# The RWKV-7 scan of layer 1: operands kept in DRAM by step, products of keys and queries by row halves, corrected values copied, states added and then scaled

## The chip, the cores and the metric

One core of one Trainium2 chip runs the whole program. The metric is the device time of one execution in microseconds (us), from the first instruction to the last. The engines are TensorE (PE; its weight loads are listed apart as PEld), VectorE (DVE), ScalarE (ACT), GpSimd (POOL) and SyncE (SP, which here issues nearly all transfers). All of it is in float32; a float32 product counts as two matmul instructions in the profile.

## What is computed

Two layers run over 512 latent tokens and 256 context tokens of width 1024. Layer 0 is attention beside a gated recurrence; layer 1 is a bidirectional RWKV-7 mixer; each has an MLP behind it. The change lies in layer 1's scan over time, which for each of 16 heads and both directions is

```python
def step(s, inp):
    r_t, w_t, kk_t, b_t, k_t, v_t = inp
    sk = jnp.einsum('bhvk,bhk->bhv', s, kk_t)
    s = s * w_t[:, :, None, :] - sk[..., None] * b_t[:, :, None, :] + v_t[..., None] * k_t[:, :, None, :]
    return s, jnp.einsum('bhvk,bhk->bhv', s, r_t)
```

over the context first and then over the latents, forward and backward, with a 64x64 state per head. Only the latent outputs are kept.

## The kernel before

The 768 tokens are cut into 12 chunks of 64. Within a chunk the recurrence is solved in closed form: a 64x64 triangular system per head and direction is inverted, and the chunks follow one another through the states. `order` gives 12 steps; step i takes one chunk forward and one backward, the first four steps over the context, the other eight over the latents. A tile holds the two directions on the two halves of the partitions, and two heads (n) per channel block; there are 8 channel blocks, `kt` 0 to 7, in two groups of four.

**Preparation** (`tm_prep`, run for 8 channel blocks by `tm_pairs`) forms the scaled keys and update vectors (`KB`), the scaled removal keys and receptances (`ql`, `qc`) and the products that the inversion starts from (`L`), and stores them in DRAM: `kbr`, `qlr`, `qcr`, `ldr`, each as one transfer from all 128 partitions. The values go to `vdr` from `tm_values`.

**The scan** (`tm_scan`) runs `tm_step(i, kt)` for the 12 steps and 8 blocks, and between the blocks of step i one piece each of

- `tm_feed(i + 1)`: loads `KB`, `QZ` and `W` of the next step, multiplies `KB` by `QZ` (16 products, `QZ` being zero where the directions don't meet), masks the result into `G` (L1082), copies the query rows of `QZ` into `G` (L1089), and transposes `KB` into `KT`;
- `tm_invert(j)`: loads `XT` from `ldr` and runs 60 multiplications and additions on `zt` and `Z` (L1124, L1125), for j in (1, 2, 4) on POOL, else on DVE; `tm_below(j)` finishes the inversion with 32x32 products.

A block of a step is a chain of small products in one PSUM tile `sc`: `G` by `W` (values over states), ACT's copy `rh`, `XT` by `rh`, DVE's predicated copy of the corrected values back into `W` (L1182), `KT` by `W`, and DVE's scaling of that sum by the decay, added to the state that POOL has already scaled (`Sd`, L1204). After each group of four blocks ACT copies the new states into the next step's `W` (L1200). Latent steps then form the outputs from `G` by `W` and `QZ` by the states.

No one writes the order of the instructions by hand: the framework's scheduler lays each engine's stream out ahead of time from its own estimates. Each engine then runs its stream in order, and a transfer is issued when SP comes to it and its buffer is free. `KB` has room for one step (two tiles of a half), `QZ` for two steps, `W` for two.

Of the kernel before, what the change touches and what calls it, by code (L numbers as in the profile page):

```python
# [15 lines left out]
P = 128  # L16
# [18 lines left out]
class Net:  # L35
# [810 lines left out]
    def tm_pairs(self, vin, lw):  # L846
# [3 lines left out]
        with self.psum("l1e") as self.pq:  # L850
# [25 lines left out]
            dec = self.sb([P, NT], F32, "L", 2)[:, :2 * KT * 12].rearrange("p (d k i) -> p d k i", d=2, k=KT)  # L876
# [67 lines left out]
    def tm_prep(self, kt, lw):  # L944
# [49 lines left out]
        for d in range(2):  # L994
# [11 lines left out]
            nc.sync.dma_start(self.kbd[d, kt], KB)  # L1006
            ql, qc = self.sb([P, 8, 128], F32, "ql", 3), self.sb([P, 4, 64], F32, "qc", 3)
            (nc.vector if kt == KT - 1 else nc.gpsimd).tensor_mul(ql[:, :, 0:64], ch(kkn)[:, 0:8], eq[:, 0:8])
            nc.gpsimd.tensor_mul(qc, ch(kkn)[:, 8:], eq[:, 8:])
            nc.gpsimd.tensor_mul(ql[:, :, 64:128], ch(r), er[:, 0:8])  # L1010
# [3 lines left out]
            qs.append((ql, qc))  # L1014
# [5 lines left out]
            yield  # L1020
        for n in range(2):
            ps = self.mm2()
            h = half(n)
            for c in range(12):
                for d in range(2):
                    o = half(1 - d)
                    x, y = KBs[d][h, c, o], qs[d][0][h, c, 0:64] if c < 8 else qs[d][1][h, c - 8]
                    self.mm(ps[o, 64 * c:64 * c + 64], *((y, x) if d else (x, y)), True, True)
            L = self.sb([P, NT], F32, "L", 2)
            nc.scalar.activation(L, ps[:, :NT], AF.Copy)  # L1030
# [20 lines left out]

    def tm_feed(self, i, KB=None, W=None):

# [4 lines left out]
        m = 128 if lat else 64  # L1058
        KB = KB or [self.sb([P, 4, 2, 128], F32, "KB", 2) for _ in range(2)]
        W = f["W"] = W or self.sb([P, KT, 2, 2, 64], F32, "W", 2)  # L1060
        QZ = f["QZ"] = self.QZ[i % 2]
        by = lambda z: z.rearrange("k (n p) m -> p (k n) m", n=2)
        flat = lambda z: z.rearrange("p k n m -> p (k n) m")
        for d in range(2):
            h = half(1 - d)
            for g in range(2):
                nc.sync.dma_start(flat(KB[g][h]), by(self.kbd[d, 4 * g:4 * g + 4, :, cs[d]]))
            nc.sync.dma_start(flat(QZ[h, :, :, d, 0:m]), by(self.qld[d, :, :, cs[d]] if lat else self.qcd[d, :, :, cs[d] - 8]))
        for d in range(2):
            v = self.vd[64 * cs[d]:64 * cs[d] + 64].rearrange("t (k n v) -> t k n v", n=2, v=64)  # L1070
            nc.sync.dma_start(W[half(d), :, d], v)
        f["G"], f["KT"] = [], []
        yield
        for g in range(4):
            ps = self.mm2()
            for j in range(2):
                for n in range(2):
                    x = 2 * m * (2 * j + n)
                    self.mm(ps[:, x:x + 2 * m], KB[g // 2][:, 2 * (g % 2) + j, n], QZ[:, 2 * g + j, n, :, 0:m], True, True)
            G = self.sb([P, 2, 2, 2, m], F32, "G", 8)  # L1080
            f["G"].append(G)
            nc.vector.tensor_mul(G.rearrange("p k n d t -> p (k n) d t"),  # L1082
                                 ps[:, :8 * m].rearrange("p (k d t) -> p k d t", d=2, t=m),
                                 self.gmask[:, :, 0:m].unsqueeze(1).to_broadcast([P, 4, 2, m]))
            if i:

                for d in range(2):
                    h = half(1 - d)
                    nc.scalar.activation(G[h, :, :, d, 0:64], QZ[h, 2 * g:2 * g + 2, :, d, 0:64], AF.Copy)  # L1089
            yield  # L1090
        for g in range(2):
            ps = self.mm2()
            for j in range(4):
                for n in range(2):
                    x = 256 * j + 128 * n
                    nc.tensor.transpose(ps[:, x:x + 128], KB[g][:, j, n], self.ident)  # L1096
            T = self.sb([P, 4, 2, 128], F32, "KT", 3, pool=self.gp)
            nc.scalar.activation(T, ps.rearrange("p (k n x) -> p k n x", k=4, n=2), AF.Copy)
            f["KT"].append(T)
            yield  # L1100

    def tm_invert(self, j):
# [3 lines left out]
        XT = self.XT[j] = self.sb([P, 2, 2, KT, 64], F32, "XT", 3, pool=self.ip)  # L1106
        for s in range(2):
            for d in range(2):
                c = self.order[2 * j + s][d]
                h = self.half(1 - d)  # L1110
                nc.sync.dma_start(XT[h, s].rearrange("p n k t -> p (n k) t"),
                                  self.ld[:, :, h, 64 * c:64 * c + 64].rearrange("n k p t -> p (n k) t"))
            for b in range(2):
                nc.vector.copy_predicated(self.GL[:, 16 * s:16 * s + 16],
                                          self.pmask[:, b].unsqueeze(1).to_broadcast([P, 16, 32]),
                                          XT[:, s, :, :, 32 * b:32 * b + 32].rearrange("p n k t -> p (n k) t"))
# [10 lines left out]
    def tm_below(self, j):  # L1127
# [3 lines left out]
        XT = XA.rearrange("p s n k t -> p (s n k) t")  # L1131
# [3 lines left out]
        units = lambda z: z.rearrange("p (n k) t -> p n k t", n=2)  # L1135
# [23 lines left out]
    def tm_step(self, i, kt):  # L1159
# [5 lines left out]
        W = f["W"][:, kt]  # L1165
        XT = self.XT[i // 2][:, i % 2]
        Q = f["QZ"][:, kt]
        G = f["G"][kt // 2][:, kt % 2]
        K = f["KT"][g][:, j]
        S, Sd = self.S[g], self.Sd[g]  # L1170
        units = [(d, n) for n in range(2) for d in range(2)]
        pr = self.ps([P, 512], "sc", 4, pool=self.sps)
        col = lambda b, d: slice(128 * b + 64 * d, 128 * b + 64 * d + 64)
        for d, n in units:
            h = half(d) if first else slice(0, P)
            self.mm(pr[half(1 - d), col(0, n)], G[h, n, d, 0:64], W[h, d, n], True, True)
        rh = self.sb([P, 2, 64], F32, "rh", 4, pool=self.gp)
        nc.scalar.activation(rh, pr[:, 0:128].rearrange("p (n v) -> p n v", n=2), AF.Copy)
        for d, n in units:
            h = half(1 - d)  # L1180
            self.mm(pr[h, col(1, n)], XT[h, n, kt], rh[h, n], True, True)
        nc.vector.copy_predicated(W, self.umask.unsqueeze(2).unsqueeze(3).to_broadcast([P, 2, 2, 64]),  # L1182
                                  pr[:, 128:256].rearrange("p (n v) -> p n v", n=2).unsqueeze(1).to_broadcast([P, 2, 2, 64]))
        if not last:
            for d, n in units:
                self.mm(pr[half(1 - d), col(2, n)], K[:, n, half(1 - d)], W[:, d, n], True, True)
            if j == 0:
                self.S2 = self.sb([P, 4, 2, 64], F32, "S", 4, pool=self.gp)
            for n in range(2):
                m = self.dec[:, n, kt, i:i + 1]  # L1190
                if first:
                    nc.vector.tensor_scalar(self.S2[:, j, n], pr[:, col(2, n)], m, None, op0=OP.mult)
                else:
                    nc.vector.scalar_tensor_tensor(self.S2[:, j, n], pr[:, col(2, n)], m, Sd[:, j, n],  # L1194
                                                   op0=OP.mult, op1=OP.add)
            if j == 3:
                W2 = self.feeds[i + 1]["W"]
                for d in range(2):
                    h = half(1 - d)
                    nc.scalar.activation(W2[h, 4 * g:4 * g + 4, d], self.S2[h], AF.Copy)  # L1200
            if j == 3 and i < len(order) - 2:
# [326 lines left out]
```

## Time and profile before

| | us |
|---|---|
| median of 3 runs | 2262.69 (2258.92 to 2269.53) |
| profiled execution | 2269.31 |
| its span | 2267.5 |
| busy in the span: PE / PEld | 2023.4 / 1619.3 |
| busy in the span: DVE / ACT / POOL | 1145.4 / 869.6 / 519.6 |
| transfers of SP's queue, share of the 16 DMA engines | 36.8% |

The span divides into layer 0 and the projections of layer 1 (to about 1210 us), the preparation (to 1375), the last value products and the first inversions (to 1466), the scan's four context steps (to 1576) and eight latent steps (to 1816), the output projection (to 1905) and the last MLP. In a row of the profile "busy" is the union of the instructions of a group, "idle before" is the engine's idle time just ahead of them with what ended most of it, and PEclk is the clock that TensorE was granted (1.0 is its upper level, 2.4 GHz; 0.5 is 1.2 GHz).

### The profile page before, as it was taken

The page shows a single profiled execution, that of the slowest core. Times are in us where ns is not written, and L with a number is a line of the kernel's source. Part 1 is how long each engine was busy: PE and PEld are TensorE (multiplying, and loading weights), DVE is VectorE, ACT ScalarE, POOL GpSimd, SP SyncE. Part 2 cuts the span into 40 slices and gives each one's busy share as a digit, 9 for nine tenths or more (in the row PEclk, how much of TensorE's full clock was granted, in tenths as well). Part 3 has the DMA queues.
Part 4 walks back from the last instruction along what each step waited for, and adds up shares of the span by engine and source line. Part 5 has one row for each costly group of instructions (what it writes and reads, how often), then busy time and mean ns, then how long its engine had stood idle before and what let it go on. Part 6 is the DMA issues. An engine that isn't in the chain of part 4 may idle for free. (4 is left out here: it accounts for less than half of the span.)

```text
span 2267.5 us, 37320 instructions
## 1 busy us (share of the span) xinstructions
PE 2023.4 (89%) x15710; PEld 1619.3 (71%) x15710; DVE 1145.4 (51%) x1835; ACT 869.6 (38%) x1333; POOL 519.6 (23%) x530
## 2 busy tenths in 40 slices
PE   5888889999999999997987769779787778999999
PEld 3666547778888888875765449667676666888887
DVE  4556664342222222328647997648575684333333
ACT  3664454231121221317744543346454432232321
POOL 0122331010010100105004983661500220110110
PEclk8999999999999999998998778889898999999999
DMA  7324441123333122212224659396644440222222
GB/s 282 119 86 136 143 164 41 37 94 119 124 129 113 56 64 67 98 42 79 93 88 148 236 223 214 71 143 102 113 91 80 76 140 19 93 93 93 93 93 93
DMA packets 231944, 248.93 MB, mean 110 GB/s; under 512 B 52448, under 2 KB 209504, under 8 KB 225376
## 3 DMA queue, kind: packets, MB, share of 16 engines
q1 hardware_dynamic: 229728, 241.30, 36.8%
q0 software_dynamic: 896, 3.15, 0.4%
q8 instruction: 123, 2.02, 0.4%
q10 hardware_dynamic: 1152, 2.10, 0.2%
q14 instruction: 45, 0.37, 0.1%
HBM read 200.82 MB, written 41.94 MB: 107 GB/s over the span
## 5 line engine op out<-in xcount | busy, mean ns | idle before, releaser
L264 ACT ACTIVATE whi<-wst 128x1024 fp32r<-128x1024 f32 x160 | 169.2, 1059 | 587.3 <-PE mm L47 567.0
L47 PE MATMUL mm<-hhi,whi 128*128 128x512 f32 (+1 forms) x992 | 346.8, 356 | 16.2 <-ACT hhi L250 6.7
L47 PE MATMUL mm<-hlo,whi 128*128 128x512 f32 (+1 forms) x992 | 352.0, 356 | 3.6 <-DVE hlo L251 3.4
L47 PE MATMUL mm<-hhi,wlo 128*128 128x512 f32 (+1 forms) x992 | 349.6, 353 | 0.0
L265 DVE TENSOR_TENSOR wlo<-wst,whi 128x1024 fp32r<-128x1024 f32 x160 | 199.9, 1251 | 255.2 <-ACT whi L264 252.4
L345 POOL TENSOR_TENSOR mp<-mr 128x768 f32<-128x768 f32 (+1 forms) x64 | 109.9, 1719 | 848.1 <-ACT mr L344 848.1
L47 PE MATMUL mm<-ahi,wlo 128*128 128x512 f32 (+1 forms) x704 | 252.9, 359 | 0.0
L47 PE MATMUL mm<-ahi,whi 128*128 128x512 f32 (+1 forms) x704 | 252.9, 360 | 0.0
L47 PE MATMUL mm<-alo,whi 128*128 128x512 f32 (+1 forms) x704 | 252.5, 359 | 0.0
L300 DVE SCALAR_TENSOR_TENSOR Xt<-mm,mod,Xt 128x512 f32<-128x512 f32 (+1 forms) x112 | 70.6, 653 | 336.8 <-PE mm L47 336.6
L47 PEld LDWEIGHTS mm<-hhi,whi 128*128 128x128 f32 x992 | 187.8, 191 | 55.2 <-ACT hhi L250 8.7
L47 PEld LDWEIGHTS mm<-hlo,whi 128*128 128x128 f32 x992 | 188.9, 190 | 32.1 <-DVE hlo L251 6.6
L47 PEld LDWEIGHTS mm<-hhi,wlo 128*128 128x128 f32 x992 | 188.4, 190 | 28.3 <-issue 0.8
L47 PEld LDWEIGHTS mm<-ahi,whi 128*128 128x128 f32 x704 | 132.2, 188 | 28.1 <-issue 6.7
L47 PEld LDWEIGHTS mm<-ahi,wlo 128*128 128x128 f32 x704 | 132.5, 188 | 22.0 <-DVE wlo L265 1.1
L47 PEld LDWEIGHTS mm<-alo,whi 128*128 128x128 f32 x704 | 132.4, 188 | 21.9
L47 PE MATMUL mm<-QZ,KB 128*128 128x256 f32 (+1 forms) x384 | 96.4, 408 | 48.1 <-DMA QZ<-qlr 20.3
L47 PEld LDWEIGHTS mm<-QZ,KB 128*128 128x128 f32 x384 | 74.1, 227 | 60.3 <-issue 26.3
L347 DVE TENSOR_TENSOR alo<-mp,ahi 128x768 fp32r<-128x768 f32 (+1 forms) x64 | 54.9, 858 | 113.1 <-ACT ahi L346 113.0
L1082 DVE TENSOR_TENSOR G<-mm,gmask 128x1024 f32<-128x1024 f32 (+1 forms) x48 | 50.2, 1047 | 88.1 <-PE mm L47 87.8
L346 ACT ACTIVATE ahi<-mp 128x768 fp32r<-128x768 f32 (+1 forms) x64 | 47.3, 739 | 110.3 <-POOL mp L345 110.3
L47 PE MATMUL sc<-W,G 128*64 128x64 f32 (+1 forms) x1280 | 67.8, 233 | 12.8 <-DVE S L1194 10.3
(462 smaller groups left out, 4207.7 us busy)
## 6 DMA issues: line engine op xcount, KB each, us to landing
wst<-in_mlp_w_dram SPq DMA_DIRECT2D x64, 1024.0 KB, 5.4
wst<-in_ada_w_dram SPq DMA_DIRECT2D x48, 1024.0 KB, 6.4
kbr<-KB SPq DMA_DIRECT2D x16, 768.0 KB, 4.5
KB<-kbr SPq DMA_DIRECT2D x48, 256.0 KB, 5.6
wst<-in_rw_w_rkv_dram SPq DMA_DIRECT2D x8, 1024.0 KB, 5.4
qlr<-ql SPq DMA_DIRECT2D x16, 512.0 KB, 3.3
QZ<-qlr SPq DMA_DIRECT2D x16, 512.0 KB, 8.8
wst<-in_hy_w_in_dram SPq DMA_DIRECT2D x7, 1024.0 KB, 5.3
```

The source lines that it names most:

```text
L47: self.nc.tensor.matmul(out, lhsT, rhs, start=start, stop=stop)
L264: nc.scalar.activation(hi, w, AF.Copy)
L265: nc.vector.tensor_sub(lo, w, hi.bitcast(F32))
L300: self.nc.vector.scalar_tensor_tensor(x, ps[:, c0:c1], self.m(l, chunk, v, kt), x, op0=OP.mult, op1=OP.add)
L345: nc.gpsimd.tensor_mul(p[:, :n], r[:, :n], r[:, :n])
L346: nc.scalar.activation(h[:, :n], p[:, :n], AF.Copy)
L347: nc.vector.tensor_sub(o[:, :n], p[:, :n], h[:, :n].bitcast(F32))
L1082: nc.vector.tensor_mul(G.rearrange("p k n d t -> p (k n) d t"), ps[:, :8 * m].rearrange("p (k d t) -> p k d t", d=2, t=m), self.gmask[:, : ...
```

## The change

1. DRAM copies are laid out by step: `kbr`, `qkr` (removal keys of all 12 chunks), `qrr` (receptances of 8) and `ldr` hold one chunk's rows of one direction together, 4 or 8 KB per partition. The loads of a step become pieces of 4 KB; the stores become pieces of 512 B (`kbr`, `ldr`) and 256 B (`qkr`, `qrr`), and those of `kbr`, `qkr` and `qrr` are issued for each half of the partitions apart. `L` has one buffer that holds both heads' parts.
2. `QZ` is split in two tiles: `A` (two buffers; removal keys on one half, masked products on the other) and `R` (receptances, with zeros on the other half). `KB` is one tile for a step, with two buffers.
3. Products of keys and queries use one half of the rows each: 32 of 64x64 for `A`, and for latent steps 32 of 64x128 for `G`. ACT's copy of the query rows is gone.
4. The corrected values are copied by ACT for one half and DVE for the other.
5. States: DVE adds the new part to the state into `T`; after each group DVE scales one half and POOL the other into the next step's `W`, and POOL scales all of it into `S`.

```diff
-            nc.sync.dma_start(self.kbd[d, kt], KB)
+            for n in range(2):
+                nc.sync.dma_start(self.kbd[d, :, :, kt, n].rearrange("c p m -> p c m"), KB[half(n)])
...
-            nc.sync.dma_start(self.qld[d, kt], ql)
-            nc.sync.dma_start(self.qcd[d, kt], qc)
+            for n in range(2):
+                nc.sync.dma_start(self.qkd[d, :, :, kt, n].rearrange("c p m -> p c m"), qk[half(n)])
+                nc.sync.dma_start(self.qrd[d, :, :, kt, n].rearrange("c p m -> p c m"), qr[half(n)])
...
-            nc.sync.dma_start(self.ld[n, kt], L)
+        nc.sync.dma_start(self.ld[:, :, kt].rearrange("c p n t -> p c n t"), L)
...
-        KB = KB or [self.sb([P, 4, 2, 128], F32, "KB", 2) for _ in range(2)]
-        QZ = f["QZ"] = self.QZ[i % 2]
+        KB = self.sb([P, KT, 2, 128], F32, "KB", 2)
+        A = f["A"] = self.sb([P, 2, KT, 2, 64], F32, "A", 2)
+        R = f["R"] = self.R[i % 2]
...
+            h, c = half(1 - d), cs[d]
+            nc.sync.dma_start(A[h, d], self.qkd[d, c])
+            for g in range(0, KT, 4):
+                nc.sync.dma_start(KB[h, g:g + 4], self.kbd[d, c, :, g:g + 4])
...
-                    self.mm(ps[:, x:x + 2 * m], KB[g // 2][:, 2 * (g % 2) + j, n], QZ[:, 2 * g + j, n, :, 0:m], True, True)
+                    self.mm(ps[half(d), x:x + 64], KB[h, k, n, half(d)], A[h, d, k, n], True, True)
...
+                            self.mm(ps[:, x:x + 64], KB[h, 4 * g + j, n], R[h, d, 4 * g + j, n], True, True)
...
-        nc.vector.copy_predicated(W, ...
+        nc.scalar.activation(W[half(1), 0], by(pr[half(1), 128:256]), AF.Copy)
+        nc.vector.tensor_copy(W[half(0), 1], by(pr[half(0), 128:256]))
...
-                    nc.vector.scalar_tensor_tensor(self.S2[:, j, n], pr[:, col(2, n)], m, Sd[:, j, n],
-                                                   op0=OP.mult, op1=OP.add)
+                nc.vector.tensor_add(self.T[:, j], by(pr[:, 256:384]), S)
...
+            for d in range(2):
+                h = half(1 - d)
+                (nc.gpsimd if d else nc.vector).tensor_mul(W2[h, d, 4 * g:4 * g + 4], self.T[h], mb[h])
+            self.S[g] = self.sb([P, 4, 2, 64], F32, "S", 4, pool=self.gp)
+            nc.gpsimd.tensor_mul(self.S[g], self.T, mb)
```

Three places of the streams show what moved. On SP, around the loads of latent step 9 (before: `KB_14359`, `QZ1`, `W_14361`) there stood

```order
L1067 DMA KB_14359<-kbr_7656 64x8x128 x2
L1067 DMA KB_14360<-kbr_7656 64x8x128 x2
L1359 DMA XT_15460<-in_rw_w_o_dram 128x8x256
L1071 DMA W_14361<-vdr_7654 64x8x128
L1068 DMA QZ1_11365<-qlr_7657 64x16x128 x2
L1071 DMA W_14361<-vdr_7654 64x8x128
```

and now, around the loads of step 8 (`A_14149`, `R0`, `W_14148`), with `KB_14558` belonging to step 9,

```order
L1068 DMA KB_14558<-kbr_7656 64x1024
L1066 DMA A_14149<-qkr_7657 64x1024 x2
L1068 DMA KB_14558<-kbr_7656 64x1024 x3
L1071 DMA R0_11375<-qrr_7658 64x1024 x2
L1072 DMA W_14148<-vdr_7654 64x1024 x2
```

`KB` is loaded a step earlier than it was; `A`, `R` and `W` are loaded where `QZ` and `W` were, and one load of `KB` stands ahead of `A`.

On PE, the products of the feed for step 9 stood among blocks of step 8 (`mm2_14397` to `mm2_14513`, each 128x256):

```order
L47 MATMUL mm2_14397<-QZ1_11365,KB_14359 128x256 x4
L47 MATMUL mm2_14433<-QZ1_11365,KB_14359 128x256 x4
L47 MATMUL sc_14522<-W_13987,G_14148 64x64 x4
L47 MATMUL sc_14522<-S_14168,QZ0_11361 64x64 x4
L47 MATMUL sc_14594<-W_13987,G_14148 64x64 x3
L47 MATMUL mm2_14442<-XN_14069,XT_12738 32x32 x32
```

and now those of the feed for step 8 (`mm2_14187`) follow the last blocks of step 6 (`sc_14061`, `sc_14088`) and the first of step 7 (`sc_14119`, `sc_14160`):

```order
L47 MATMUL sc_14088<-W_13258,A_13259 64x64 x4
L47 MATMUL sc_14119<-W_13669,A_13670 64x64 x4
L47 MATMUL sc_14160<-W_13669,A_13670 64x64 x4
L47 MATMUL sc_14061<-rh_14066,XT_12073 64x64 x4
L47 MATMUL sc_14088<-rh_14093,XT_12073 64x64 x4
L47 MATMUL sc_14119<-rh_14124,XT_12073 64x64 x4
L47 MATMUL sc_14160<-rh_14165,XT_12073 64x64 x4
L47 MATMUL sc_14061<-W_13258,KT_13499 64x64 x4
L47 MATMUL mm2_14187<-A_14149,KB_14147 64x64
```

The first row is the last read of `A_13259`, whose buffer `A_14149` takes over; 28 products stand between it and the first that needs `A_14149`.

On POOL, among the operations of inversion 2, the scaled states stood early and apart:

```order
L1124 TENSOR_TENSOR zt_11469<-Z_11467 128x234
L1204 TENSOR_TENSOR Sd_11604<-S_11444,dec_7666 128x512
L1125 TENSOR_TENSOR Z_11467<-Z_11467,zt_11469 128x18x13
```

and now the first pair of them stands behind 43 of the 60 operations:

```order
L1130 TENSOR_TENSOR zt<-Z 128x198
L1217 TENSOR_TENSOR W<-T,dec 64x512
L1219 TENSOR_TENSOR S<-T,dec 128x512
L1131 TENSOR_TENSOR Z<-Z,zt 128x9x22
```

The first stood behind 25 of the 60 operations before. In inversion 4 the pairs now stand behind 29 operations and behind all 60.

## Rows read from the trace of the kernel before

**Rows 1.** Busy time by stage: length, then PE, PEld, DVE, ACT, POOL, PEclk, DMA share, GB/s.
```profile
1210.00:1375.00 165.00, 122.34 (x1331) 86.46 (x1330) 147.50 (x100) 88.84 (x114) 128.14 (x101) 0.76 0.61 221
1466.00:1576.00 110.00, 91.16 (x1551) 78.06 (x1549) 63.44 (x164) 58.83 (x124) 44.36 (x72) 0.89 0.87 141
1576.00:1816.00 240.00, 191.33 (x3672) 161.58 (x3672) 153.39 (x382) 111.31 (x242) 59.32 (x79) 0.89 0.48 85
```
**Rows 2.** Chain of waits within 1466 to 1830 us, shares by line.
```profile
by line: PE mm L47 25.4%; PE sc L47 15.9%; DMA QZ<-qlr 11.1%; DMA KB<-kbr 7.3%; PE mm L1096 4.7%; issue 4.7%; DMA XT<-ldr 4.4%; DVE G L1082 2.9%; POOL Z L1125 2.0%; POOL zt L1124 1.7%; SPq L1071 1.7%; DVE W L1182 1.6%; DVE gn L196 1.5%; DVE
```
**Rows 3.** What PE waited for, 1452 to 1818 us: us in total, times, longest.
```profile
PE mm L47 <- DMA QZ<-qlr: 20.3, 4, 7.8
PE mm L47 <- issue: 11.6, 2, 8.1
PE sc L47 <- DVE S L1194: 10.3, 7, 4.5
PE mm L47 <- POOL Z L1125: 8.3, 1, 8.3
PE mm L47 <- DMA KB<-kbr: 6.8, 4, 2.8
```
**Rows 4.** Groups of instructions: busy us, mean ns | idle before.
```profile
L47 PE MATMUL mm<-QZ,KB 128*128 128x256 f32 (+1 forms) x384 | 96.4, 408 | 48.1 <-DMA QZ<-qlr 20.3 <-issue 11.6 <-POOL Z L1125 8.3
L47 PE MATMUL sc<-rh,XT 64*64 64x64 f32 x768 | 41.3, 232 | 2.6 <-issue 1.5 <-ACT rh L1178 0.8
L47 PEld LDWEIGHTS sc<-rh,XT 64*64 64x64 f32 x768 | 30.6, 137 | 11.1 <-issue 5.3 <-ACT rh L1178 1.7 <-ACT XT L1156 0.3
L1089 ACT ACTIVATE G<-QZ 64x256 f32<-64x256 f32 x88 | 36.5, 415 | 102.2 <-DVE G L1082 101.2
L1200 ACT ACTIVATE W<-S 64x512 f32<-64x512 f32 x44 | 27.6, 628 | 7.4 <-DVE S L1194 5.1 <-DMA W<-vdr 1.4 <-DVE S L1192 0.4
L1204 POOL TENSOR_TENSOR Sd<-S,dec 128x512 f32<-128x512 f32 x20 | 21.3, 1066 | 172.6 <-DVE S L1194 162.9 <-DVE zt L1124 5.1 <-DMA W<-vdr 4.6
```
**Rows 5.** Transfers by line: count, KB each, median us from issue to landing.
```profile
kbr<-KB SPq DMA_DIRECT2D x16, 768.0 KB, 4.5
KB<-kbr SPq DMA_DIRECT2D x48, 256.0 KB, 5.6
qlr<-ql SPq DMA_DIRECT2D x16, 512.0 KB, 3.3
QZ<-qlr SPq DMA_DIRECT2D x16, 512.0 KB, 8.8
qcr<-qc SPq DMA_DIRECT2D x16, 128.0 KB, 3.4
```
**Rows 6.** Issue of KB's loads on SP: duration ns, shortest/median/longest.
```profile
L1067 SPq DMA_DIRECT2D KB<-kbr x48: 573/627/3726, 1405.0 to 1776.8; - x48
```
**Rows 7.** Transfers from 1690 to 1710 us in 40 slices of 0.5 us.
```profile
DMA  1000026999999999999999999999999999999983
GB/s 33 0 0 0 0 62 198 331 204 210 147 194 236 188 228 212 179 262 315 350 344 352 341 222 172 164 222 197 176 172 173 184 232 182 174 176 192 200 138 55
```
**Rows 8.** Busy time from the first store of the preparation to the last, columns as rows 1.
```profile
1219.00:1374.00 155.00, 113.58 (x1306) 81.30 (x1306) 141.14 (x93) 81.84 (x105) 125.41 (x98) 0.76 0.64 232
```
**Rows 9.** Timeline: QZ's issue on SP and the products behind it on PE.
```profile
1696.76 4.08 SPq L1068 DMA_DIRECT2D QZ<-qlr  x2
...
1710.21 6.59 PE L47 MATMUL mm<-QZ,KB 128*128 128x256 f32 x16 [5.54 <-DMA QZ<-qlr]
```
**Rows 10.** Timeline of POOL, inversion 2.
```profile
1467.57 0.25 POOL L1124 TENSOR_TENSOR zt<-Z 128x30 f32<-128x30 f32 x1
...
1500.09 1.06 POOL L1204 TENSOR_TENSOR Sd<-S,dec 128x512 f32<-128x512 f32 x1 [1.39 <-DVE S L1194]
...
1504.51 0.53 POOL L1124 TENSOR_TENSOR zt<-Z 128x198 f32<-128x198 f32 x1
...
1518.08 0.25 POOL L1125 TENSOR_TENSOR Z<-Z,zt 128x30 f32<-128x30 f32 x1
```

More of the change, by code (lines that the diff above doesn't have):

```diff
@@ L1087, in tm_feed @@
+        for k in range(KT):
+            for n in range(2):
                 for d in range(2):
                     h = half(1 - d)
[L1089 to L1091 removed]
+                    x = 64 * (2 * k + n)
+                    self.mm(ps[half(d), x:x + 64], KB[h, k, n, half(d)], A[h, d, k, n], True, True)
+        for d in range(2):
+            h = half(d)
+            nc.vector.tensor_mul(A[h, d].rearrange("p k n t -> p (k n) t"), ps[h].rearrange("p (k t) -> p k t", t=64),
+                                 self.gmask[h, 0:1].to_broadcast([64, 16, 64]))
@@ new lines, in tm_feed @@
+        yield
+        if lat:
+            G = f["G"] = self.sb([P, 2, 2, 8, 64], F32, "G", 2)
+            for g in range(2):
+                ps = self.mm2()
+                for j in range(4):
+                    for n in range(2):
+                        for d in range(2):
+                            h = half(1 - d)
+                            x = 512 * d + 64 * (2 * j + n)
+                            self.mm(ps[:, x:x + 64], KB[h, 4 * g + j, n], R[h, d, 4 * g + j, n], True, True)
+                nc.vector.tensor_mul(G[:, g], ps.rearrange("p (d k t) -> p d k t", d=2, t=64),
+                                     self.gmask[:, 1:3].unsqueeze(2).to_broadcast([P, 2, 8, 64]))
+                yield
@@ L1092, in tm_feed @@
+        T = f["KT"] = self.sb([P, KT, 2, 128], F32, "KT", 2, pool=self.gp)
+        for g in range(0, KT, 4):
             ps = self.mm2()
@@ L1218, in tm_step @@
         if j == 3 and not last:
-            self.S[g] = self.S2
+            m = self.dec[:, :, 4 * g:4 * g + 4, i].rearrange("p n k -> p k n")
+            mb = m.unsqueeze(3).to_broadcast([P, 4, 2, 64])
+            W2 = self.feeds[i + 1]["W"]
+            for d in range(2):
+                h = half(1 - d)
+                (nc.gpsimd if d else nc.vector).tensor_mul(W2[h, d, 4 * g:4 * g + 4], self.T[h], mb[h])
+            self.S[g] = self.sb([P, 4, 2, 64], F32, "S", 4, pool=self.gp)
+            nc.gpsimd.tensor_mul(self.S[g], self.T, mb)
     def tm_post(self, l, parts=1):
@@ L1317, in layer1 @@
         self.rd = dram("rdr", [KT, P, NL])
-        self.kbd = dram("kbr", [2, KT, P, 12, 128])
-        self.qld, self.qcd = dram("qlr", [2, KT, P, 8, 128]), dram("qcr", [2, KT, P, 4, 64])
-        self.ld = dram("ldr", [2, KT, P, NT])
+        self.kbd = dram("kbr", [2, 12, 64, KT, 2, 128])
+        self.qkd, self.qrd = dram("qkr", [2, 12, 64, KT, 2, 64]), dram("qrr", [2, 8, 64, KT, 2, 64])
+        self.ld = dram("ldr", [12, P, KT, 2, 64])
         self.hlb = cp.tile([P, 4, KT], F32, name="hlb")
@@ L1491, in layout @@
     t = np.arange(64)[None, :]
-    gm = np.zeros((P, 2, P), np.float32)
-    for d in range(2):
-        gm[:, d, :64], gm[:, d, 64:] = (half == d) & (i > t if d else i < t), (i >= t if d else i <= t)
-    r["gmask"] = gm
+    r["gmask"] = np.stack([np.where(half == 0, i < t, i > t), i <= t, i >= t], 1)
     r["smask"] = np.tile(t > 0, (P, 12))
@@ L1502, in layout @@
     r["pmask"] = np.stack([(b == j) & (i < t) for j in range(2)], 1).astype(np.int32)
-    r["umask"] = np.stack([p // 64 == 1 - d for d in range(2)], 1).astype(np.int32)
     return r
```

124 lines of the change are left out of this document (42 added, 82 removed).

## The prediction, as it went on record

> **What bounds the kernel now.** I read the stages first [rows 1]. The change touches two of them: the preparation (1210 to 1375 us) and the scan (1466 to 1816). In the preparation VectorE is busy for 147.5 of 165 us, POOL for 128.1 and the DMA engines for 61% of the time; PE is far from full. In the scan's latent steps it is PE that is busy, 191.3 of 240 us, while VectorE has 153 and ACT 111. In the context steps the DMA engines are at 87%, though they move 141 GB/s only. Then the chain of waits over the scan [rows 2]: some 46% of the listed shares are PE's own products, 11% are loads of `QZ` and 7% loads of `KB`. So the scan is bound by PE's stream and by the operands that it waits for. The waits of PE give the sizes [rows 3]: 20.3 us for `QZ` in 4 waits, 11.6 us "issue" in 2, 6.8 us for `KB`. Last, one such stall on the timeline [rows 9]: SP issues the two loads of `QZ` at 1696.8, and PE stands 5.5 us idle before the 16 products that need them. The group of these products [rows 4] has 384 instructions, 96.4 us busy and 48.1 us idle before them. That is the one group in the scan with such a sum, and the change rewrites it.
>
> **The sum is made against the profiled execution**, 2269.3 us (span 2267.5 and 1.8 outside). The median of the three runs, 2262.7, lies 6.6 lower; I apply the differences to the median. About 0.5%, 11 us, is what a measurement here can tell from no change.
>
> **1. Products of keys and queries.** Removed: 384 instructions, 96.4 us busy [rows 4]. Added: 12 feeds of 32 products for `A` and 8 of 32 for `G`, each two instructions, so 768 + 512 = 1280, of 64 columns. No such shape stands in the old feed; the nearest are the 64x64 products of `XT` by `rh`, 41.3 us busy for 768, or 53.8 ns each, and their weight loads, 30.6 us for 768, or 39.8 ns each [rows 4]. 1280 at these prices is 51 to 69 us. I take 45 ns, since weight loads and products overlap: 58 us. All of it is on the path, as PE's stream is. Term: -38 (-27 to -45).
>
> **2. Waits for loads.** The three waits above are 38.7 us [rows 3]; I count the issue wait because its two places are just ahead of these products. `KB` comes a step earlier and has two buffers, so its wait goes. `A` stays late: its buffer is free after the last products of the step two before, and the order puts one `KB` load ahead of its two halves. These are 3 x 256 KB, all into half of the partitions. In the slices of 1690 to 1710 [rows 7] loads into 64 partitions run at 147 to 236 GB/s while the DMA engines are full, and a whole-tile load between them at 315 to 352. At 200 GB/s, 768 KB take 3.9 us; a single load of 256 KB lands 5.6 us after issue [rows 5], so I take 5.6. PE has 28 products, 56 instructions, in between: 2.5 us at 45 ns. About 3 us of stall are left for each of 9 feeds, 27 us in all. Term: -12. The bounds are -39 (the order of the blocks covers the load) and 0 (each stall as long as today). SP itself is no hindrance: a `KB` load's issue takes 0.6 us, at worst 3.7 [rows 6].
>
> One rule bears on the rate. Rows 7 show half tiles at about 200 GB/s and a whole tile at 350, but these also differ in the length of their pieces. The Trainium skill, "SBUF — State Buffer", section "Door 1: The DMA port swizzle (why [64,N] ≈ [32,N])", says that a range of 64 partitions reaches half of the DMA ports; by that rule the 4-KB pieces change nothing in rate and the term stays -12. Were it the 512-B pieces that slow today's loads, 768 KB at 350 GB/s would take 2.2 us, all of it beside the 28 products but for the time to issue, and the term would be nearer -30.
>
> **3. States on POOL.** Before, POOL scaled the state ahead of need (`Sd`, 1066 ns each [rows 4]), and DVE's last operation gave the new state. Now DVE adds, and scaling comes after: `W` by POOL on one half and DVE on the other, then `S` by POOL. So the next step waits for POOL's place in its stream. In latent steps without an inversion on POOL this costs what it saves: ACT's copy was 628 ns for half a tile [rows 4] and goes. While inversion 2 runs it does not. Its 60 operations run from 1467.6 to 1518.1, the old `Sd` stood at 1500.1 [rows 10], and the first pair now stands behind the 43rd, which ended at 1505.0, 1504 without the old `Sd`. The states of group 0 are there at about 1499. So step 1 starts some 5 us later, and the pair itself adds 2: +7. In inversion 4 the pairs stand behind 29 operations and behind all 60, with more time between: +3. Term: +10 (0, if PE has other products to do, to +25, if both inversions push a half-step out).
>
> **4. Stores of the preparation.** From first store to last are 155 us, with DVE busy for 141 [rows 8]. The DMA engines are busy for 0.64 x 155 = 99 us and move 232 GB/s x 155 us = 36 MB, or 363 GB/s while they work. The old stores of `kbr` are 768 KB, of `qlr` 512 and of `qcr` 128, sixteen of each, landing in 3.3 to 4.5 us [rows 5]. Now 16 x 1408 KB = 23.1 MB leave as half tiles in pieces of 256 and 512 B. Priced as half-tile loads, 200 GB/s [rows 7], they take 115 us, the other 12.9 MB 36 us: 151 of 155 us. That nearly fills the stage, and a buffer of `KB` comes free later. At 170 GB/s it is 171 us, 30 more than DVE's 141, and 16 longer than the stage. If both halves go at once, 363 GB/s holds and nothing changes. Nothing shown is a store of half a tile, so I take +12 (0 to +30). SP issues 104 stores instead of 64, 65 us of 155 at 0.63 us: no bound.
>
> **5. At nothing.** ACT loses 36.5 us of copies of queries and 27.6 of states [rows 4] and gains a half copy per block, at most 0.4 us each, like the copies of queries: it has 111 of 240 us and hides it. DVE's predicated copy becomes a plain one of half the size, two scaled additions become one, and a scaling per group is added; it has 153 of 240 [rows 1]. These do lie in a block's chain, but four blocks are in flight.
>
> Sum: -38 - 12 + 10 + 12 = **-28**, 2241 against the profiled execution's 2269, **2235** against the median.
>
> **Rivals.** *(a) All of it hides.* Term 1 at -45, waits -30 to -39, POOL and stores at nothing: -75 to -84, or -64 with term 1 as taken and two thirds of the waits gone. For it: the order gives PE a step's blocks to do while `A` comes. Against it: rows 9, where the blocks did not suffice. About 2195; chance 0.18.
>
> *(b) It balances.* The POOL pairs cost +25 and the stores +25, against -50: about 2262. For it: POOL's stream is in order, and the first group of step 1 is read by everything behind it. Chance 0.16.
>
> *(c) Slower, by the small stores.* `qkr` and `qrr` are 16 x 640 KB = 10.5 MB in pieces of 256 B. If these move at 100 GB/s, half the rate of the half-tile loads, they take 105 us instead of 52, and the preparation is 52 us longer: -28 + 52 = +24, 2287. It turns at 130 GB/s, where the extra is 28 us. Against it: `QZ`'s and `KB`'s loads of short pieces are limited to about 200 only [rows 7], and nothing here stores so. The Trainium skill, "DMA: Bandwidth & Descriptors", section "Specifications", asks for transfers of at least 512 B for line rate and says that below this the engine reads, modifies and writes; by that rule this rival would hold, and no run so far shows a store of 256 B. Chance 0.16.
>
> That the change does not do what it says is mostly excluded: the order has `KB` a step earlier and the query copies gone. What it doesn't do is bring `A` earlier, which is in term 2.
>
> **How the numbers follow.** The case forecast has 0.50, (a) 0.18, (b) 0.16, (c) 0.16. The ends of its four terms lie 7, 27, 10 and 12 us below the values taken and 11, 12, 15 and 18 above; all at one end at once is unlikely, so I add them as squares, 32 and 28, and take two thirds: the forecast case runs from 2214 to 2254, and nearly all of it is faster by 0.5%. So faster has 0.50 + 0.18 = 0.68, the same 0.16, slower 0.16. The range is to leave out 2 in 10 at most: it takes in (b) and most of (a), down to 2188, and goes up to 2275, leaving out (c) and (a)'s lower end.
>
> **What the profile after would show.** Right: the products of `KB` with `A` and `R` at 51 to 69 us busy; no wait of PE for `KB`, and waits for `A` of some 3 us a feed; the stage from 1466 shorter by about 40 us, the preparation longer by about 12. A step 1 that starts late, with PE or ACT waiting for POOL's `W`, would confirm term 3. Wrong: products at over 75 us (term 1); waits for `A` as long as `QZ`'s were, or none (term 2); a preparation as long as before, or over 30 us longer with DVE waiting for stores to release buffers (term 4 and rival c); ACT or DVE named ahead of PE's products in place of loads (part 5).

## The result, and the profile after

The change makes the kernel slower: 2343.94 us (2335.98 to 2351.48, 4 runs) against 2260.81 of the kernel before; the ratio is 1.0364 [1.0313, 1.0415]. Forecast were 2235 us and a range of 2188 to 2275. The profiled execution has a span of 2345.5 us, 78.0 more than before.

Where it went is read by stages, cut at the same events in both kernels: last store of `ldr`, first product of a scan step, first product of the states in a latent step, the last one, last `o`. Busy time by stage of the kernel before (length, PE, PEld, DVE, ACT, POOL, PEclk, DMA share, GB/s; first, second and last of the five; the two between, the context and the latent steps, are those of [rows 1] to within 0.4 us):

```profile
1200.00:1371.00 171.00, 125.05 (x1312) 87.45 (x1311) 149.60 (x102) 89.85 (x116) 128.60 (x108) 0.76 0.60 217
1371.00:1466.70 95.70, 80.11 (x902) 78.59 (x900) 69.10 (x94) 25.19 (x33) 48.21 (x71) 0.89 0.55 120
...
1816.20:1868.90 52.70, 37.61 (x394) 36.22 (x390) 43.34 (x81) 19.00 (x26) 12.71 (x4) 0.90 0.46 151
```

The same five of the changed kernel:

```profile
1200.00:1379.50 179.50, 125.49 (x1396) 94.00 (x1396) 157.19 (x105) 89.18 (x116) 106.19 (x92) 0.75 0.81 201
1379.50:1481.50 102.00, 77.02 (x860) 74.98 (x858) 63.65 (x89) 25.22 (x32) 49.55 (x83) 0.87 0.47 122
1481.50:1613.40 131.90, 89.97 (x1650) 77.71 (x1651) 67.78 (x156) 41.05 (x100) 49.81 (x68) 0.72 0.51 118
1613.40:1888.40 275.00, 230.13 (x4418) 202.56 (x4416) 144.05 (x313) 93.02 (x229) 76.35 (x93) 0.77 0.31 74
1888.40:1946.80 58.40, 44.84 (x399) 42.42 (x395) 42.70 (x82) 19.01 (x26) 17.76 (x5) 0.80 0.42 136
```

Preparation +8.5, inversions +6.3, context steps +22.0, latent steps +35.4, tail (to the last `o`) +5.7: 77.9 us. In the latent steps PE is 39 us busier than before (230 against 191), at a granted clock of 0.77 instead of 0.89, and waits about as long in all (44.8 us, 47.7 before). The context steps lose their time in another way: the clock is 0.72 instead of 0.89, but PE is no busier (90.0 us, 91.1 before), and its waits grow from 18.7 to 41.8 us. The DMA engines are less busy in the scan than before (0.51 and 0.31; 0.87 and 0.48 in [rows 1]).

PE's groups over the scan, 1478 to 1890 us (busy us, mean ns | idle before), matmuls and then two weight loads:

```profile
L47 PE MATMUL mm<-R,KB 64*128 64x64 f32 x512 | 53.1, 349 | 6.5 <-DMA R<-qrr 5.1 <-ACT PL L1150 1.4
L47 PE MATMUL sc<-rh,XT 64*64 64x64 f32 x768 | 48.0, 263 | 8.2 <-ACT rh L1182 7.6 <-issue 0.5
L47 PE MATMUL mm<-A,KB 64*64 64x64 f32 x766 | 40.0, 248 | 24.7 <-DMA A<-qkr 17.6 <-DMA KB<-kbr 7.1
```

```profile
L47 PEld LDWEIGHTS mm<-R,KB 64*128 64x128 f32 x512 | 46.9, 252 | 10.3 <-DMA R<-qrr 5.7 <-ACT PL L1150 1.5
L47 PEld LDWEIGHTS mm<-A,KB 64*64 64x64 f32 x764 | 33.0, 157 | 26.6 <-DMA A<-qkr 16.4 <-issue 6.0 <-ACT rh L1182 1.4
```

The new products take 40.0 + 53.1 = 93.1 us, the old 96.4 [rows 4]: next to nothing is gained. And `XT` by `rh`, 768 instructions that the change does not touch, take 48.0 us where they took 41.3 [rows 4]. Added up over all such untouched groups of the scan (`rh`, `KT`, `W` by `A` or `G`, the states, the transposes, the three 32x32 ones) it is 290.7 us after and 239.7 before: 51 us for the same work. Some 37 of it lie in the latent steps and 11 in the context steps, where the feeds' products fall by 10 (from 34.0 to 24.1 us) and so make up for it.

What PE waited for in the same stretch (us in total, times, longest):

```profile
PE mm L47 <- DMA A<-qkr: 17.6, 11, 3.5
PE sc L47 <- POOL W L1217: 13.3, 1, 13.3
PE mm L47 <- DVE A L1083: 10.2, 2, 5.2
PE sc L47 <- DVE W L1187: 8.5, 10, 4.8
PE sc L47 <- DVE T L1196: 7.8, 8, 3.1
PE sc L47 <- ACT rh L1182: 7.6, 9, 2.0
PE mm L47 <- DMA KB<-kbr: 7.1, 3, 3.5
PE mm L47 <- DMA R<-qrr: 5.1, 4, 2.0
```

POOL's `W` of the second row lies in the context steps. All rows of that view together are 89 us, and were 67 before. Waits for the loads of these products are 17.6 + 7.1 + 5.1 = 29.8 us; they were 38.7 [rows 3].

The clock is best seen in short pieces around a stall. PE of the kernel before, pieces of 7 us (length, PE busy, PEclk, DMA share, GB/s), around the stall of [rows 9]:

```profile
1702.00:1709.00 7.00, 1.12 (x27) 0.77 1.24 187
1709.00:1716.00 7.00, 5.79 (x14) 0.50 0.10 18
1716.00:1723.00 7.00, 7.00 (x137) 1.00 0.01 2
```

and of the changed kernel around the feed of step 8:

```profile
1683.00:1690.00 7.00, 5.86 (x134) 0.87 1.04 226
1690.00:1697.00 7.00, 5.74 (x64) 0.62 0.26 59
1697.00:1704.00 7.00, 7.00 (x130) 0.50 0.01 2
1704.00:1711.00 7.00, 7.00 (x68) 0.50 0.01 2
1711.00:1718.00 7.00, 5.80 (x108) 0.50 0.00 0
1718.00:1725.00 7.00, 3.52 (x76) 0.93 0.68 181
```

Before, PE came out of an idle stretch at 0.50, ran the products of `QZ` by `KB` at that clock, and was at 1.00 in the next piece. After, waits of 1.7 and 0.7 us for `R` (at 1689 and 1692) are followed by three whole pieces at 0.50, with PE busy for 19.8 of the 21 us. It is not this place alone: with the latent steps cut into such pieces, one of 34 lies at 0.50 throughout before, and nine of 39 after. In seven of the nine PE is busy for 6.5 us or more; before, four pieces had it busy for 0.7 to 1.1 us only, and each time the clock was at 1.00 two pieces later.

### The profile page after: what moved, and what is told of

It is laid out like the page before. It is cut to its first block, busy times and chain, and to the rows that moved or that the text cites. A ratio compares the mean times of both kernels' runs of the same rounds, so it can differ in the third digit from the quotient of the medians.

```text
span 2345.5 us, 38943 instructions
## 1 busy us (share of the span) xinstructions
PE 2068.9 (88%) x16606; PEld 1673.1 (71%) x16606; DVE 1143.3 (49%) x1761; ACT 834.0 (36%) x1297; POOL 527.4 (22%) x538
## 5 line engine op out<-in xcount | busy, mean ns | idle before, releaser
L1217 POOL TENSOR_TENSOR W<-T,dec 64x512 f32<-64x512 f32 x22 | 27.7, 1257 | 208.7 <-DVE T L1196 123.6
L1187 DVE COPY W<-sc 64x128 f32<-64x128 f32 x96 | 25.9, 279 | 83.3 <-ACT W L1186 80.5
L47 PE MATMUL sc<-W,A 128*64 128x64 f32 (+1 forms) x768 | 47.1, 254 | 20.7 <-POOL W L1217 13.3
L47 PE MATMUL mm<-vx,whi 128*128 128x512 f32 (+1 forms) x168 | 60.6, 363 | 3.9 <-DVE vx L368 3.8
```

What stands on the lines that cost most here:

```text
L47: self.nc.tensor.matmul(out, lhsT, rhs, start=start, stop=stop)
L1187: nc.vector.tensor_copy(W[half(0), 1], by(pr[half(0), 128:256]))
L1217: (nc.gpsimd if d else nc.vector).tensor_mul(W2[h, d, 4 * g:4 * g + 4], self.T[h], mb[h])
```

## The experiments

Every kernel ran beside the kernel before on one chip; the ratio is to that. The trials ran in four groups on four chips (k1 to k4, k5 to k11, k12, k13 and k14), so a small difference between groups is read from the ratios. Clock and length are those of the context and of the latent steps; "untouched" is the sum named above.

| kernel | median us | ratio, 95% | clock | length us | untouched us |
|---|---|---|---|---|---|
| before | 2260.81 | 1 | 0.89, 0.89 | 110, 240 | 239.7 |
| changed | 2343.94 | 1.0364 [1.0313, 1.0415] | 0.72, 0.77 | 132, 275 | 290.7 |
| k1_rfull | 2293.65 | 1.0134 [1.0114, 1.0154] | 0.73, 0.91 | 132, 222 | 262.9 |
| k2_bhalf | 2332.65 | 1.0314 [1.0283, 1.0344] | 0.60, 0.78 | 160, 255 | 289.8 |
| k3_wdve | 2350.09 | 1.0393 [1.0369, 1.0417] | 0.73, 0.74 | 127, 294 | |
| k4_ln | 2344.94 | 1.0360 [1.0338, 1.0382] | 0.73, 0.78 | 130, 268 | |
| k5_fill | 2357.32 | 1.0436 [1.0407, 1.0465] | 0.76, 0.86 | 138, 280 | 271.3 |
| k6_layout | 2284.28 | 1.0112 [1.0096, 1.0127] | 0.73, 0.92 | 125, 225 | |
| k7_w1 | 2293.55 | 1.0148 [1.0133, 1.0163] | 0.74, 0.91 | 127, 225 | |
| k8_ctx | 2287.89 | 1.0125 [1.0109, 1.0140] | 0.86, 0.86 | 108, 248 | |
| k9_prep | 2269.40 | 1.0042 [1.0029, 1.0054] | 0.76, 0.94 | 122, 217 | |
| k10_prep_ctx | 2248.94 | 0.9951 [0.9933, 0.9968] | 0.86, 0.91 | 100, 216 | 243.7 |
| k11_prep_ctx_w | 2251.10 | 0.9959 [0.9941, 0.9976] | 0.88, 0.91 | 97, 219 | |
| k12_pred | 2259.05 | 0.9987 [0.9971, 1.0003] | 0.82, 0.91 | 111, 224 | |
| k13_rows | 2360.88 | 1.0437 [1.0416, 1.0459] | 0.71, 0.80 | 137, 281 | 278.6 |
| k14_cols | 2336.79 | 1.0344 [1.0307, 1.0382] | 0.72, 0.80 | 133, 276 | 282.4 |

**k1_rfull: `R`'s products over all rows.**

```diff
-                        for d in range(2):
-                            self.mm(ps[:, x:x + 64], KB[h, 4 * g + j, n], R[h, d, 4 * g + j, n], True, True)
+                        self.mm(ps[:, x:x + 128], KB[:, 4 * g + j, n], R[:, :, 4 * g + j, n], True, True)
...
```

> The changed kernel, with the products of KB by R made over all 128 rows again (R has zeros on the other half): 16 products of 128x128 by 128 columns a feed in place of 32 of 64x128 by 64. Measured now: 512 instructions, 53.1 us busy. By the nearest row of the kernel before (128x128 by 128 columns, 20.8 us for 128 instructions) 256 of them cost 42 us. Theory 1 (the granted clock, 0.77 in the latent steps against 0.89 before, fell because narrow products do not bring it back after a stall): the clock of the latent steps rises to 0.82 or more, the other products of the scan shorten with it, and the total is 20 to 40 us lower. Theory 2 (the clock follows the stalls, whatever the products): the clock stays at 0.75 to 0.79 and the total falls by the 11 us of the products or less.

PE's groups, 1478 to 1840 us:

```profile
L47 PE MATMUL sc<-W,KT 128*64 128x64 f32 x704 | 44.4, 264 | 9.3 <-DVE W L1185 9.3
L47 PE MATMUL sc<-rh,XT 64*64 64x64 f32 x768 | 43.6, 246 | 4.8 <-ACT rh L1180 4.8
L47 PE MATMUL mm<-R,KB 128*128 128x128 f32 x256 | 42.6, 327 | 10.0 <-DMA R<-qrr 8.4 <-DVE G L1094 1.7
```

Theory 1 holds, and by more than it gave: 50 us less, of which the products themselves are 10.5 (42.6 for 53.1) and the untouched ones 28. The latent steps are now 18 us shorter than in the kernel before; only the context steps, whose own feeds have none but `A`'s half products, keep their 0.73.

**k2_bhalf: the kernel before, with `QZ`'s products by halves and nothing else.**

```diff
-                    self.mm(ps[:, x:x + 2 * m], KB[g // 2][:, 2 * (g % 2) + j, n], QZ[:, 2 * g + j, n, :, 0:m], True, True)
+                    for d in range(2):
+                        h, x = half(1 - d), 512 * d + m * (2 * j + n)
+                        self.mm(ps[:, x:x + m], KB[g // 2][h, 2 * (g % 2) + j, n], QZ[h, 2 * g + j, n, d, 0:m], True, True)
...
```

> The kernel before, with only its products of KB by QZ split by row halves, each half without the other's zeros: 768 instructions of 64x128 (512 by 128 columns, 256 by 64) in place of 384 of 128x128. Nothing else is changed: layout, states, POOL, copies, loads. Theory 1 (narrow products leave the clock low): the latent steps' clock falls from 0.89 to below 0.84, the same other products take at least 10 us more, and the total rises by 15 to 50 us. Theory 2 (the clock follows the stalls): the clock stays within 0.02 of 0.89 and the total moves by no more than the products themselves, 80 to 110 us against 96, so by -16 to +14.

Its context and latent steps:

```profile
1465.50:1625.30 159.80, 129.82 (x1690) 110.04 (x1690) 75.56 (x192) 58.87 (x123) 43.66 (x72) 0.60 0.55 96
1625.30:1880.70 255.40, 196.89 (x3900) 174.90 (x3898) 143.43 (x353) 110.44 (x243) 56.06 (x78) 0.78 0.46 82
```

Theory 1 again, above its upper end: +69 us from this one edit. The untouched products take 50 us more; PE's waits for `QZ` and `KB` grow too, from 27 to 48 us, so not all of it is the clock. Old layout, old states, old loads: changing them is not needed to lose the clock.

**k3_wdve** gives VectorE all of `W`'s scaling (`nc.vector.tensor_mul(W2[...])` for both halves).

> The changed kernel, with the half of the next step's W that POOL scales given to VectorE, which scales the other half already; POOL keeps the scaled S. Theory 1 (POOL's place behind the operations of inversion 2 holds up step 1): PE's wait of 13.3 us for POOL's W goes, step 1 starts earlier, and the total falls by 8 to 18 us. Rival (VectorE is then in the way: two half tiles of about 1 us each at the end of a group, before the next step can start): the wait shows under VectorE's W instead, and the total stays within 6 us or rises, to +15.

Over 1478 to 1905 us the first row of PE's waits is

```profile
PE mm L47 <- DMA A<-qkr: 28.6, 13, 10.1
```

The wait for POOL's `W` is gone, as theory 1 wanted, and the time is not: the context steps are 5 us shorter, 11 us more is waited for `A`, the latent clock is 0.74, and the total is that of the changed kernel to within the intervals. The rival's number is right, though not its place.

**k4_ln** makes `L` two tiles, stored apart.

> The changed kernel, with L in two tiles again, one for each head of the block with its own store (384 KB in pieces of 256 B in place of 768 KB in pieces of 512 B). Theory 1 (the preparation is longer because ACT's L waits for the store of the one buffer, 9.0 us, and PE for ACT's L, 16.2 us): the preparation ends 6 to 9 us earlier and the total falls by as much. Rival (the stores themselves, with the DMA engines at 0.81 instead of 0.60, fill the stage): the waits move to KB or the keys, and the total stays within 4 us or rises, to +10, as more of the stores are of 256 B.

The total stays as it was, and the last store of `ldr` comes at 1393.0 instead of 1379.5, the first scan product at 1488.0 instead of 1481.5. So the rival has the total; the one buffer of `L` was no hold-up to gain from.

**k5_fill** adds useless work:

```diff
                 ps = self.mm2()
+                for q in range(4):
+                    self.mm(ps[:, 256 * q:256 * q + 256], KB[:, 4 * g + q, 0], KB[:, 4 * g + q], True, True)
```

> The changed kernel as it is, with useless work added: ahead of each of the 16 groups of KB by R, 4 products of KB by KB, 128x128 by 256 columns, whose result is overwritten; 128 instructions in all. By the row of such products in the kernel before (75.6 us for 256) they cost 38 us. Theory 1 (the granted clock stays low after a stall while only narrow products follow): the clock of the latent steps rises from 0.77 to 0.85 or more, the others' time shrinks by 20 to 50 us, and the total moves by -12 to +15. Theory 2 (the clock has nothing to do with the width): the clock stays below 0.80 and the total rises by 30 to 60 us.

```profile
L47 PE MATMUL mm<-KB 128*128 128x256 f32 x128 | 48.7, 535 | 1.5 <-ACT PL L1152 1.5
L47 PE MATMUL sc<-rh,XT 64*64 64x64 f32 x768 | 44.8, 247 | 3.1 <-ACT rh L1184 3.1
L47 PE MATMUL mm<-R,KB 64*128 64x64 f32 x512 | 43.3, 297 | 6.0 <-DMA R<-qrr 6.0
```

The clock rises to 0.86. The useless products take 48.7 us; the untouched ones take 19 us less and `A` and `R` 12 less, with not a column of theirs changed. PE's waits in the latent steps are 44.1 us, as in the changed kernel (44.8), so that the clock did not rise for want of stalls. The total is 13 us up by the medians and 16 by the ratios: theory 1, at the upper end of its range or just over it.

**k6_layout** is k1 with the DRAM layout of the kernel before: stores from all 128 partitions, `L` in two tiles, loads in short pieces.

> The version with R's products over all rows (2293.7 us), and with the DRAM copies laid out by block again: every store of KB, keys, receptances and L from all 128 partitions in pieces of 1.5 to 6 KB, L in two tiles; the loads in pieces of 256 and 512 B. Theory 1 (the stores of half tiles in short pieces make the preparation 12 us longer): the preparation is 8 to 14 us shorter and the total falls by 5 to 14; the loads, whose median landing times hardly differ between the kernels (5.6 and 5.8 us for KB), cost at most 8 us more in the scan. Rival (the short-piece loads are worse than the stores were: 256-B pieces for A and R): the scan gets longer by 10 us or more and the total is the same or up to 15 us higher.

The total falls by 9 us (5 by the ratios, whose intervals overlap), but the preparation does not give it: `ldr`'s last store is at 1380.0, in k1 at 1383.5, though the DMA share of that stage falls from 0.80 to 0.57. Both theories miss on the place.

**k7_w1** is k1 with `W` on VectorE after steps 0 and 1 (`nc.gpsimd if d and i > 1 else nc.vector`).

> The version with R's products over all rows (2293.7 us), with W's half that POOL scales given to VectorE after steps 0 and 1 alone, where inversion 2 occupies POOL. Theory 1 (PE's wait of 14.4 us for W there is on the path and only there does POOL hold up): the context steps shorten by 6 to 14 us and the total falls as much. Rival (what comes next, POOL's S behind the same operations or the loads, ends as late): the wait changes its name and the total moves by less than 4 us.

The rival: the context steps shorten by 4.9 us, PE's wait for `A` is 22.5 us instead of 9.5, the total is the same.

**k8_ctx** is k1 with the context steps' products over all rows.

```diff
             nc.sync.dma_start(A[h, d], self.qkd[d, c])
+            if not lat:
+                nc.sync.dma_start(R[h, d], self.qkd[d, c])
...
+                        self.mm(ps[:, x:x + 128], KB[:, 4 * g + j, n], R[:, :, 4 * g + j, n], True, True)
...
```

> The version with R's products over all rows (2293.7 us), with the context steps' products of KB by the removal keys made over all rows too: the keys are also loaded into R (zeros on the other half, idle in these steps; 512 KB more a step), and 16 products of 128x128 by 128 columns take the place of 32 of 64x64 by 64; VectorE masks the half of each result that is wanted. Theory 1 (the context steps' clock of 0.73, against 0.89 before, comes from the narrow products): their clock rises to 0.80 or more and the total falls by 5 to 20 us, though 32 instructions at 162 ns cost 2 us a feed more than 64 at 52 ns. Theory 2 (the clock there comes from the wait for POOL's W and for loads): it stays below 0.78, and the total moves by 0 to +12.

The context steps come out as theory 1 said: clock 0.86, 108 us instead of 132. But their PE is as busy as in k1 (86.8 us, 88.2 there), and what they lose in length is waits: 20.4 us instead of 43.5, with 0.8 for POOL's `W` instead of 14.4. POOL's first pair now stands behind 39 of the 60 operations of inversion 2, and stood behind 43 in k1. So whether the products or the new order raised this clock is not shown. The latent steps lose 26 us, and the tail is 10 shorter, since more of it now runs among them; 6 us are left by the medians and 2 by the ratios, which is not clear of noise. Every edit makes the scheduler lay the streams out anew, so a small total after a large local gain says little by itself.

**k9_prep, k10_prep_ctx, k11_prep_ctx_w.** k9 is k6 with `ql` and `qc` formed and stored as before the change; k10 adds the edit of k8, k11 that of k7.

> The version with R's products over all rows and the DRAM copies by block (2284.3 us), with the preparation's keys and receptances formed as before the change too: ql and qc by three POOL operations a direction (512, 256 and 512 elements) and stored as two tiles; the scan loads A from ql or qc and R from the other half of ql, in pieces of 256 B. Theory 1 (the preparation's remaining 9 us over the kernel before come from how qk and qr are formed and ordered, not from stores): the preparation is 6 to 10 us shorter and the total falls by as much, to 2274 to 2279. Rival (they come from elsewhere, the later values or the scan's first loads): the total stays within 4 us of 2284.

> The same, with the context steps' products over all rows as well (keys loaded into R too). Theory 1 (the width of the products sets how soon the clock comes back; what the latent steps lost in the earlier trial of this came from another order of the work): the context steps keep a clock of 0.83 or more and some 105 to 112 us, and the total is 8 to 25 us below the run without it. Rival (what the context steps gain the latent steps lose again): total within 6 us of the run without it.

> The same again, with W's half that POOL scales given to VectorE after steps 0 and 1. Theory 1 (with the clock up, POOL's place behind inversion 2 is on the path): 3 to 12 us below the run without it. Rival (the wait changes its name, as in the first trial): within 3 us.

The preparation of k9, and the context and latent steps of k10:

```profile
1200.00:1371.10 171.10, 124.67 (x1312) 87.44 (x1311) 149.78 (x103) 89.75 (x116) 128.69 (x108) 0.76 0.60 217
```

```profile
1474.50:1574.80 100.30, 82.37 (x1555) 73.67 (x1554) 64.86 (x152) 40.14 (x101) 43.58 (x57) 0.86 0.90 155
1574.80:1790.50 215.70, 185.83 (x4170) 166.09 (x4168) 150.69 (x321) 92.47 (x228) 79.18 (x95) 0.91 0.52 99
```

In k9 the preparation is back at its 171 us, 9 less than in k6, so its extra came from forming `qk` and `qr` and the order that follows. The total falls by 15, more than theory 1's 6 to 10. k10 gains 20 more, the size that theory 1 gave, and at 0.9951 is faster than both kernels. As in k8 its context steps are shorter by waits (17.5 us, 40.3 in k9) and not by PE's work (82.4 us, 81.8 in k9), and the order has moved: POOL's first `W` stands behind 47 of the 60 operations in k9 and behind 41 in k10, where POOL itself waits for the state.

```profile
1501.79 1.05 POOL L1218 TENSOR_TENSOR W<-T,dec 64x512 f32<-64x512 f32 x1
```

```profile
1494.89 1.56 POOL L1233 TENSOR_TENSOR W<-T,dec 64x512 f32<-64x512 f32 x1 [0.32 <-DVE T L1210]
```

So k10 shows what the whole set of edits is worth, and not that the width of the context steps' products gives the 20 us. k11 makes no difference, as the rival has it; but PE no longer waits for POOL's `W` in k10, so that nothing was left for this edit to take away.

**k12_pred** is k10 with the predicated copy back.

> The fastest version so far (products over all rows in both kinds of steps, preparation as before the change, 2248.9 us), with the corrected values copied as before the change: one predicated copy by VectorE (442 ns in the kernel before) in place of a copy by ACT (271 ns) and one by VectorE (279 ns) that starts after it. Theory 1 (the copy lies in each block's chain, and PE waits for VectorE's half, 5.4 us in 8 waits): undoing it changes that wait by a few us either way, total within 5 us. Rival (VectorE, at 150 of 216 us in the latent steps, becomes the hold-up with 96 copies 160 ns longer, 15 us in all): the total rises by 6 to 15 us.

The rival, with 10 us by the medians and 8 by the ratios: the split copies, which the prediction put at nothing, are worth about that here.

**k13_rows and k14_cols** take k1's edit apart: all rows with 64 columns, half the rows with 128 columns.

```diff
+                            self.mm(ps[:, x:x + 64], KB[:, 4 * g + j, n], R[:, d, 4 * g + j, n], True, True)
...
```

```diff
+                            self.mm(ps[:, x:x + 128], KB[h, 2 * g + j, n], R[h, :, 2 * g + j, n], True, True)
...
```

> The changed kernel, with the products of KB by R over all 128 rows but each direction by itself: 32 of 128x128 by 64 columns a feed, as many as now (32 of 64x128 by 64). Theory 1 (it is the half of the rows that leaves the clock low): the latent steps' clock rises from 0.77 to 0.85 or more and the total falls by 25 to 50 us, near the 2293.7 of the version with 16 products by 128 columns. Theory 2 (it is the 64 columns): the clock stays below 0.80 and the total stays within 10 us of 2343.9.

> The changed kernel, with the products of KB by R over one half of the rows as now, but each by 128 columns, 64 of them R's zeros whose result is left unread: 32 of 64x128 by 128 columns a feed, and VectorE masks in four pieces more. Theory 1 (half of the rows leaves the clock low): the latent steps' clock stays below 0.80 and the total is the same or up to 25 us higher, for the wider products. Theory 2 (64 columns leave it low): the clock rises to 0.85 or more and the total falls by 10 us or more.

`R`'s products in k13, and in k14:

```profile
L47 PE MATMUL mm<-R,KB 128*128 128x64 f32 x512 | 89.1, 343 | 8.9 <-DMA R<-qrr 7.5 <-ACT PL L1150 1.4
```

```profile
L47 PE MATMUL mm<-R,KB 64*128 64x128 f32 x512 | 62.3, 370 | 22.4 <-DMA R<-qrr 10.6 <-DVE A L1083 9.9 <-DVE gn L195 1.6
```

Neither property alone is enough: either one brings the latent clock to 0.80, both together (k1) to 0.91. The stalls do not make this difference, since PE waits for 29.5 us in the latent steps of k13 and for 29.3 in those of k1. The total of k13, 17 us above the changed kernel, fits neither theory; that of k14, 7 below, is not clear of noise. One rival is left: both trials have 512 instructions, as the changed kernel, and k1 has 256, so the shape of the products is not told apart from their number and that of the weight loads. And both trials cost more PE time than k1's 42.6 us for the same result.

## Why the prediction was wrong

**Term 1, the products (-38): the step that failed first.** It priced all 1280 instructions at 45 ns from products of 64x64 weights. `A`'s came out at 40.0 / 766 = 52 ns, inside the bounds. `R`'s have weights of 64x128, load in 46.9 / 512 = 92 ns against 33.0 / 764 = 43, and cost 104 ns each: 53 us where 23 had been put. The nearest row for these was the other form of the old group, 128x128 by 128 columns: 20.8 us for 128 instructions, 162 ns. Half the rows and half the columns together cut a product from 166 ns (k1) to 104, but two of them do the work of one and take 208. So the products took 93.1 us, above the 75 that the prediction had named as the sign against this term, and it came to -3 instead of -38. Part of this is the low clock itself: `R`'s cost 85 ns each in k5, and `A`'s 23.2 / 512 = 45 ns in k10, at latent clocks of 0.86 and 0.91.

**The missing term, the clock (+51).** [Rows 1] show 0.89 and [rows 9] a feed that runs behind a stall. The sum took every unchanged product at its old duration, and no rival had a clock that changes, though the change replaces the very products that ran while the clock came back. The untouched products grew by 51 us, against 78 in all. The 37 of them in the latent steps are on the path, as PE's busy time grew there by 39 and its waits did not. The 11 in the context steps are not shown to be, since PE was no busier there. k2 shows that the half products alone lose the clock, k1 that undoing them for `R` gives 50 us back, k5 that whole products which compute nothing raise the clock too.

**Term 2, the loads (-12).** About right: 29.8 us of waits for 38.7, with `A` at 17.6. `KB`'s did not go (7.1), and `R` brought 5.1. The half-tile loads run at 226 GB/s in pieces of 4 KB with the DMA share at 1.04, and ran at 187 with 1.24 (one stretch of 7 us each): better, and far from the 350 of a whole tile [rows 7]. The Trainium skill, "SBUF — State Buffer", section "Door 1: The DMA port swizzle (why [64,N] ≈ [32,N])", says that a range of 64 partitions reaches half of the ports; the trace agrees in so far as the longer pieces did not bring half tiles near the rate of a whole one.

**Term 3, POOL (+10).** The wait is there, in one piece of 13.3 us at the start of step 1, where it was put, and PE's waits make up the context steps' 22 us. But k3 and k7 take this wait away, shorten those steps by 5 us and gain nothing in all: a wait of 10 to 11 us for `A` stands in its place. It had hidden the loads behind it. In k8 and k10 it goes with another order of POOL's stream, and nothing takes its place.

**Term 4, the stores (+12), and rival (c).** The preparation is 8.5 us longer, near the term, but by luck: the reason is another. Whole-tile stores (k6) left it within 3.5 us of k1's; forming `ql` and `qc` as before (k9) brought it back. So neither the half tiles nor the 256-B stores were its limit: the DMA share did rise to 0.81, but with 0.57 in k6 the stage is as long. Slower came true, by a mechanism that was none of the rivals.

**Part 5 (nothing)** missed the gain of the split copies, 8 to 10 us in k12.

What stays open: why the latent steps of k8 lost 26 us; what in the order of the preparation costs its 8.5 us; the 12 us of the inversions and the tail; how much of the context steps' low clock is due to the products and how much to the waits; and whether it is the shape of the products or their number that the clock goes by. Moving `A`'s load ahead with a third buffer was not tried.

## What to carry to other kernels

Halving the rows and columns of a TensorE product saved nothing here, since weight loads and instructions doubled (2 x 104 ns against 166); price a new product by the row with its weights' shape, not by one with its columns. Where the profile shows a granted clock below 1, ask which products run while it comes back, and treat their removal as a cost on everything behind them. With the whole products, the old DRAM layout and the old preparation back, and the rest of the change kept, the kernel ended below both, at 0.9951 [0.9933, 0.9968].

## What was not expected of the hardware

A busy PE did not bring its clock back: from 1697 to 1711 us it is busy for 14 of 14 us at a granted 0.50, its lower level of 1.2 GHz. The Trainium skill, "TensorE: Matmul & The Clock Gate", section "What's actually happening", says that the gate follows how busy PE has recently been; by the profile's busy time the trace does not agree. The profile models where a product ends, so its busy time does not show how full the array was. What the runs show is the clock of the latent steps beside the products of `R`: 0.77 with half the rows and 64 columns, 0.80 with all rows or with 128 columns, 0.91 with both and half as many products (k1), and 0.86 when whole products that compute nothing are put ahead of the first kind (k5).
